# Where the second layer's residual gets its first norm's weights: inside the last output projection, or ahead of it by way of memory

## The chip, the core and the metric

The kernel runs on one core of one Trainium2 chip. The core has engines that each work through their own queue in order: PE (matmuls; PEld is its weight load), DVE (VectorE), ACT (ScalarE) and POOL (GpSimd). SP issues most DMAs, in order too; POOL issues some. The metric is the device time of one execution in microseconds (us), as a median over runs.

## The reference, cut to what matters

Two layers, each a mixer with three groups of heads and a norm behind it. 1024 tokens of 1024 values.

```
for l in range(2):
    mod = silu(c) @ w_ada[l] + b_ada[l];  shift, scale, gate = split(mod, 3)
    h = x * (1 + scale) + shift
    p = h @ w_in[l]              # latents of MLA, q k v of the dilated and the sparse heads, indexer, gates
    y = concat(MLA heads, dilated heads, sparse heads) * silu(p_gate)
    x = layer_norm(ALPHA * x + (1 + gate) * (y @ w_out[l]), ln_g[l], ln_b[l])
```

`layer_norm` takes mean and variance over the 1024 values of a token, then multiplies by `ln_g` and adds `ln_b`. The x that enters the second layer's sum is the normed x of the first layer *with* its weights: n*ln_g[0] + ln_b[0], where n is the value before weights.

## The kernel before, in words

Tokens are cut into 8 blocks of 128 (tb 7 down to 0, the order TBO). Each float32 operand is split into a high and a low part, and a product is three matmuls (high·high, low·high, high·low). A layer runs: `indexer` (keys and queries of the indexer, scores into `acc`), the dilated heads with the selection of keys beside them, the sparse heads, the latent (MLA) heads in `mla`, and `out_proj`. At the end of the first layer's `out_proj` the normed blocks n are stored to `x1_d[tb]`, transposed on PE (L876), scaled and shifted with weights folded in (`mod_h`, L366 to L371) to become h of the second layer; `mod_h` gives the low part of every odd k to POOL (L371). The stages that follow (values of the dilated heads, L377 to L384, then the indexer, from L393) read that h. The low parts of the weights that they multiply by come from POOL too (L192), and POOL issues the DMAs that copy the indexer's key to the other 64 partitions (`dup_k`, L235, L236).

In the second layer's `out_proj` (`last`), each block's n comes back from `x1_d[tb]` into a buffer of the ring XR (two buffers, L803), POOL multiplies it by ln_g[0] and adds ln_b[0] (L841, L842), PE forms the block in two halves of 512 columns of 24 matmuls each (L198), and DVE does, by halves: times the gate (L854), plus ALPHA times the residual (L855), statistics (L856); then by blocks the mean and variance (L858, L860), POOL the power (L861), DVE the norm with its weights (L865, L866), and SP the store (L867). Four sum buffers (ring X, L833) and five PSUM banks stand between PE and DVE.

The instructions are not issued in program order. A scheduler (`schedule_with_timeline_sim`, L1061) simulates the program and gives each engine a list; an instruction whose inputs are early may stand early in its engine's list, whatever its place in the text. Between engines, semaphores order the work. The names of tiles are in the views without their numbers: `acc` is the region that the rings XR and X use, `g` the other XR buffer, `bi` in L854 the gate.

Of the kernel before, what the change touches and what calls it, by code (L numbers as in the profile page):

```python
# [8 lines left out]
F32 = mybir.dt.float32  # L9
# [4 lines left out]
OP = mybir.AluOpType  # L14
# [7 lines left out]
P = 128  # L22
NB = 8
# [12 lines left out]
TBO = (7,6,5,4,3,2,1,0)  # L36
# [24 lines left out]
KE = (1,1)  # L61

NPL = 2

EARLY = (2,2)
FB = ((0,2,4,0,2,0),(1,3,1,1,1,1))
# [40 lines left out]
def trunk(ctx: ExitStack, tc: tile.TileContext, a, out):  # L107
    nc = tc.nc
    pe, act, dve, pool, sp = nc.tensor, nc.scalar, nc.vector, nc.gpsimd, nc.sync

    sb = ctx.enter_context(tc.tile_pool(name="sb", bufs=1))
# [5 lines left out]
    dr = ctx.enter_context(tc.tile_pool(name="dr", bufs=1, space=DRAM))  # L117
# [6 lines left out]
    def fresh(tag, dtype, n=1024):  # L124

        return sb.tile([P, n], dtype, name=tag, tag=tag, bufs=1)
# [4 lines left out]
    PR3 = [fresh(f"pr{i}", F32) for i in range(3)]  # L131
    PR = Halves(PR3)
    BI = Ring(fresh(f"bi{i}", F32) for i in range(2))
    G = Ring(fresh(f"g{i}", F32) for i in range(2))
    RW = Ring(fresh(f"rw{i}", F32, 512) for i in range(2))
    acc = sb.tile([P, IDX_TOT], F32, name="acc")
    AC = [acc[:, IDX_TOT - (i + 1) * 1024:IDX_TOT - i * 1024] for i in range(4)]
    scrf = sb.tile([P, 512], F32, name="scr")
    scr, scr8 = [scrf[:, i * 256:i * 256 + 256].bitcast(mybir.dt.uint8) for i in range(2)]
    o_ps = ps_o.tile([P, 2, 256], F32, name="O")  # L140

    ident = sb.tile([P, P], F32, name="ident")
    causb = sb.tile([P, 512], BF16, name="causb")
    dist2 = sb.tile([P, 2 * P], BF16, name="dist2")
# [34 lines left out]
    kr_d = dr.tile([32, 1024], F32, name="kr_d")  # L179
    g1_d = [dr.tile([1, 1024], F32, name=f"g1_d{i}") for i in range(DEPTH)]  # L180
    x1_d = [dr.tile([P, 1024], F32, name=f"x1_d{i}") for i in range(NB)]


    def bc(t):
        return t.bitcast(F32)
# [177 lines left out]
    def vblk(h):  # L363
        return lambda kb: VS[0][:, h * 1024 + kb * P:h * 1024 + (kb + 1) * P]
# [178 lines left out]
    def heads_bc(l, first, nh, gate0, y0, fill, extra=None):  # L543
# [23 lines left out]
        for h in range(nh):  # L567
            if extra:
                bias, scale = chosen, SLOPES[6 + h]
                if h == NPL:  # L570
                    PR.tiles = PR3[:]
# [105 lines left out]
    def mla(l, values):  # L677
# [8 lines left out]
        def slots(h):  # L686

            rows = [PR.tiles[(5 * h + turn.index(i)) % len(PR.tiles)] for i, _ in place]
            return [r[:, o:o + (qb + 1) * P] for qb, (r, (_, o)) in enumerate(zip(rows, place))]
# [18 lines left out]
        def keys(p):  # L708
            wh, wl = split_w(a["wuk"][l, p], 256)

            def evac(half, cols, ps):
                dve.tensor_tensor(kraw[:, cols], ps, rb[half], OP.mult)
            project(wh, wl, 2, CK, evac)
# [41 lines left out]

            project(wh, wl, 6, CA, evac)

        q, y = {}, {}
        keys(0)
        key(0)  # L760
        query(0)
# [4 lines left out]
        for h in range(6):  # L766
            if h % 2 == 0:
                y[h // 2] = G.next()
                sp.dma_start(y[h // 2], ga_d[h // 2])
            Kh, Kl = KA[h % 2]  # L770
            Qh, Ql = q[h]

            def done(g, yt=y[h // 2], yo=HA[h // 2], c=None):
                c = c or slice(g * 256, g * 256 + 256)
                act.activation(yo[0][:, c], yt[:, c], AF.Copy)
                pool.tensor_tensor(yo[1][:, c], yt[:, c], bc(yo[0][:, c]), OP.subtract)

            attend(f'A{h}', [(Qh, Kh), (Ql, Kh), (Qh, Kl)], vblk((h + 4) % 6), None, scq, y[h // 2],
                   (h % 2) * 64, ORDA[l], done if h in (3, 5) else None, PACK[l] and slots(h))
            if h < 4:  # L780
                if h % 2 == 0:
                    keys(h // 2 + 1)
                    if h == 2:
                        done(0, y[0], HA[0], slice(0, 1024))
                key(h + 2)
            for i in range(NQ[l][h], NQ[l][h + 1]):
                if i < 5:
                    query(i)

    def out_proj(l):  # L790
        last = l == DEPTH - 1
        order = [3, 4, 5, 6, 7, 0, 1, 2]
        Y = HA
        for k in order[:5]:
            raw = WR.next()
            sp.dma_start(raw, y_d[k])
            act.activation(Y[k][0], raw, AF.Copy)
            (pool if k in YP[l] else dve).tensor_tensor(Y[k][1], raw, bc(Y[k][0]), OP.subtract)


        Vs = [VS[0][:, i * 1024:(i + 1) * 1024] for i in range(6)]
        f = G.n % 2 ^ 1
        XR = Ring([AC[0]] + ([G.tiles[f]] if last else []))  # L803
        at = {3: (Vs[4], Vs[5]), 4: (Vs[0], Vs[1]), 5: W.tiles[0:2], 6: W.tiles[2:4],
              7: (fresh(f"g{1 - f}", F32R), fresh("bi1", F32R)), 0: held[0:2], 1: held[2:4],
              2: (Vs[2], [fresh(f"rw{n}", F32R, 512) for n in range(2)])}
        wo = {}
        for k in order:
            raw = WR.next()
            sp.dma_start(raw, a["w_out"][l, k])  # L810
            hi, lo = at[k]
            eng = pool if k in WP[l] else dve
            for n in range(2):
                c = slice(n * 512, n * 512 + 512)
                act.activation(hi[:, c], raw[:, c], AF.Copy)
                eng.tensor_tensor(lo[n] if k == 2 else lo[:, c], raw[:, c], bc(hi[:, c]), OP.subtract)
            wo[k] = [(hi[:, n * 512:n * 512 + 512], lo[n] if k == 2 else lo[:, n * 512:n * 512 + 512]) for n in range(2)]
        g1 = BI.tiles[0]
        sp.dma_start(g1, g1_d[l].to_broadcast([P, 1024]))
        lgb = []  # L820
        if last:
            for t, src in zip([fresh("pt0", F32), fresh("pt1", F32), PR3[2], PR3[1]],
                              (a["ln_g"][0], a["ln_b"][0], a["ln_g"][1], a["ln_b"][1])):
                sp.dma_start(t, src.to_broadcast([P, 1024]))
                lgb.append(t)
        else:

            lnc = small.tile([P, 2, 8], F32, name="lnc", bufs=1)
            sp.dma_start(lnc, a["ln_c"])
            dve.tensor_tensor(lnc[:, 0, :], lnc[:, 0, :], scale1_n, OP.mult)  # L830
            dve.tensor_tensor(lnc[:, 1, :], lnc[:, 1, :], scale1_n, OP.mult)
            dve.tensor_tensor(lnc[:, 1, :], lnc[:, 1, :], shift_n, OP.add)
        X = Ring(AC[1:4] + [PR3[0]])  # L833
        PR.tiles = [G.tiles[f]]
        xs = {}
        for tb in TBO:
            tok = slice(tb * P, (tb + 1) * P)
            xr = XR.next()
            sp.dma_start(xr, x1_d[tb] if last else a["x"][tb])
            if last:  # L840
                pool.tensor_tensor(xr, xr, lgb[0], OP.mult)  # L841
                pool.tensor_tensor(xr, xr, lgb[1], OP.add)  # L842
            r = X.next()
            st = small.tile([P, 2, 6], F32, name="st")
            for n in range(2):
                cols = slice(n * 512, n * 512 + 512)
                ps = (ps_p if n else ps_s).tile([P, 512], F32, name="pj" if n else "S")
                items = []
                for k in order:
                    yh, yl = Y[k]  # L850
                    w0, w1 = wo[k][n]
                    items += [(yh[:, tok], w0), (yl[:, tok], w0), (yh[:, tok], w1)]
                chain(ps, items)
                dve.tensor_tensor(r[:, cols], ps, g1[:, cols], OP.mult)  # L854
                dve.scalar_tensor_tensor(r[:, cols], xr[:, cols], ALPHA, r[:, cols], OP.mult, OP.add)  # L855
                dve.bn_stats(st[:, n, :], r[:, cols])  # L856
            mv = small.tile([P, 2], F32, name="mv")
            dve.bn_aggr(mv, st)  # L858
            rs = small.tile([P, 1], F32, name="rs")
            dve.tensor_scalar(rs, mv[:, 1:2], 1e-5, None, OP.add)  # L860
            pool.tensor_tensor(rs, rs, mhalf, OP.pow)  # L861
            if last:
                for n in range(2):
                    cols = slice(n * 512, (n + 1) * 512)
                    dve.scalar_tensor_tensor(r[:, cols], r[:, cols], mv[:, 0:1], lgb[2][:, cols], OP.subtract, OP.mult)  # L865
                    dve.scalar_tensor_tensor(r[:, cols], r[:, cols], rs, lgb[3][:, cols], OP.mult, OP.add)  # L866
                    sp.dma_start(out[tb][:, cols], r[:, cols])  # L867
                continue
            dve.tensor_scalar(r, r, mv[:, 0:1], rs, OP.subtract, OP.mult)
            sp.dma_start(x1_d[tb], r)  # L870
            xs[tb] = r
            if len(xs) == 4:
                for k in range(8):
                    t = ps_t.tile([P, 512], F32, name="T")
                    for j in range(4):
                        pe.transpose(t[:, j * P:(j + 1) * P], xs[tb // 4 * 4 + j][:, k * P:(k + 1) * P], ident)  # L876
                    mod_h(t, tb // 4, k, PR.next(), lnc[:, 0, :], lnc[:, 1, :])
                xs = {}
# [186 lines left out]
```

## Time and profile before

| | us |
|---|---|
| median of 3 runs | 1823.04 (1819.21 to 1823.08) |
| the profiled execution | 1825.06 |
| its span, first to last instruction | 1823.3 |
| busy in the span: PE, DVE, ACT, POOL | 1676.4 (92%), 1446.8 (79%), 1022.5 (56%), 696.9 (38%) |
| mean granted TensorE clock | 0.972 of full |

How to read it: the shares are means over stages with different limits. Near the end of the span the share of PE falls and that of POOL rises, which the forty slices of the page show as `PE ...8993` and `POOL ...6264`; ACT is at 0 in the last slices. For what a change in one stage is worth, that stage alone is read: who waits there, and for whom.

### The profile page before, as it was taken

What the parts mean: (1) busy time and instruction counts of PE and PEld (TensorE: products, weight loads), DVE (VectorE), ACT (ScalarE), POOL (GpSimd) and SP (SyncE); (2) the same over time, 40 slices, a digit from 0 to 9 for tenths busy, and PEclk for the clock granted to TensorE, in tenths of its full rate; (3) what the DMA queues carried; (4) which work ended last, traced back from release to release, by engine and by line L of the source; (5) the groups of instructions that cost most, each with busy time, mean ns of one, the idle gap of its engine ahead of it and who ended that gap; (6) DMA issues with size and microseconds to landing.
All of it is one profiled execution on the core that took longest, in us unless ns stands there. A gap on an engine that the chain in (4) does not pass through costs nothing. (4 is left out here: it accounts for less than half of the span.)

```text
span 1823.3 us, 26916 instructions
## 1 busy us (share of the span) xinstructions
PE 1676.4 (92%) x9080; PEld 1446.7 (79%) x9080; DVE 1446.8 (79%) x3510; ACT 1022.5 (56%) x2010; POOL 696.9 (38%) x625
## 2 busy tenths in 40 slices
PE   4889898999989999989999989999999899998993
PEld 4777677888887889868899978877789788986882
DVE  8889799985779678985773679999577967788589
ACT  3244477789643666575122646877974357767500
POOL 3421133333343455473322213223334346566264
PEclk9899999999999999999999999999999999999997
DMA  8465112233202441222331121232221225113222
GB/s 338 148 213 185 47 47 70 99 111 98 77 25 71 146 161 45 71 81 90 119 127 50 62 66 36 81 116 78 74 93 47 73 94 204 53 54 99 80 102 95
DMA packets 55366, 178.94 MB, mean 98 GB/s; under 512 B 7606, under 2 KB 8630, under 8 KB 54716
## 3 DMA queue, kind: packets, MB, share of 16 engines
q1 hardware_dynamic: 50812, 147.86, 24.2%
q0 software_dynamic: 4416, 29.36, 5.5%
q8 instruction: 72, 1.18, 0.3%
q14 instruction: 66, 0.54, 0.1%
HBM read 129.74 MB, written 34.87 MB: 90 GB/s over the span
## 5 line engine op out<-in xcount | busy, mean ns | idle before, releaser
L198 PE MATMUL pj<-h,w 128*128 128x512 f32 (+1 forms) x3408 | 840.0, 393 | 19.0 <-DVE qk L232 10.0
L198 PEld LDWEIGHTS pj<-h,w 128*128 128x128 f32 x3408 | 632.7, 191 | 138.2 <-issue 13.9
L198 PE MATMUL S<-qk,qk 128*128 128x512 f32 (+2 forms) x1104 | 284.1, 360 | 16.4 <-DVE mx L282 10.2
L192 POOL TENSOR_TENSOR w<-wr,w 128x1024 fp32r<-128x1024 f32 (+2 forms) x86 | 192.3, 2238 | 272.4 <-ACT w L191 258.5
L292 POOL TENSOR_SCALAR pr<-pr,den 128x896 f32<-128x896 f32 (+7 forms) x180 | 139.1, 776 | 285.4 <-DVE den L291 234.2
L318 DVE TENSOR_TENSOR pt<-T,pt 128x512 fp32r<-128x512 f32 (+1 forms) x320 | 199.8, 632 | 43.9 <-ACT pt L317 38.5
L481 ACT ACTIVATE scr<-acc,thr 128x768 uint8<-128x768 f32 x186 | 193.2, 1039 | 70.7 <-DVE thr L477 64.8
L317 ACT ACTIVATE pt<-T 128x512 fp32r<-128x512 f32 (+1 forms) x320 | 172.4, 552 | 104.4 <-PE T L314 46.3
L326 PE MATMUL O<-pt,v 128*128 128x256 f32 (+1 forms) x1280 | 215.8, 287 | 16.0 <-DVE pt L318 9.8
L198 PEld LDWEIGHTS S<-qk,qk 128*128 128x128 f32 x1104 | 184.3, 190 | 43.0 <-DVE mx L282 14.6
L326 PEld LDWEIGHTS O<-pt,v 128*128 128x128 f32 x1280 | 187.2, 192 | 36.2 <-DVE pt L318 14.8
L333 POOL TENSOR_TENSOR g<-g,osum 64x256 f32<-64x256 f32 x128 | 98.7, 771 | 224.9 <-DVE osum L331 223.4
L290 ACT ACTIVATE pr<-pr,mx 128x384 f32<-128x384 f32 (+7 forms) x188 | 145.5, 775 | 54.0 <-DVE mx L282 41.0
L461 DVE TENSOR_SCALAR_CACHE_REDUCE scr<-acc,thr 128x384 uint8<-128x384 f32 (+3 forms) x204 | 156.2, 766 | 3.2
L314 PE MATMUL T<-ident,pr 128*128 128x128 f32 x852 | 146.0, 279 | 9.2 <-POOL pr L292 5.4
L191 ACT ACTIVATE w<-wr 128x1024 fp32r<-128x1024 f32 (+2 forms) x86 | 83.9, 977 | 63.6 <-PE pj L198 58.2
L314 PEld LDWEIGHTS T<-ident,pr 128*128 128x128 f32 x852 | 102.4, 142 | 21.3 <-POOL pr L292 6.6
L198 PE MATMUL pj<-w,h 128*128 128x256 f32 (+2 forms) x672 | 108.9, 303 | 2.9 <-DVE g L241 2.0
L198 PEld LDWEIGHTS pj<-w,h 128*128 128x128 f32 x672 | 93.0, 193 | 8.0 <-DVE g L241 2.2
L435 DVE SCALAR_TENSOR_TENSOR acc<-S,wi,acc 128x512 f32<-128x512 f32 (+1 forms) x84 | 56.2, 678 | 30.7 <-ACT S L430 30.4
L330 ACT ACTIVATE osum<-O 64x256 f32<-64x256 f32 x128 | 48.6, 380 | 51.4 <-PE O L326 46.3
L282 DVE CUSTOM_DVE_ANT_0 pr<-S,bi 128x384 f32<-128x384 f32 (+2 forms) x96 | 52.2, 552 | 25.6 <-PE T L314 15.7
(274 smaller groups left out, 2625.3 us busy)
## 6 DMA issues: line engine op xcount, KB each, us to landing
wr<-in_wt_dram SPq DMA_DIRECT2D x62, 512.0 KB, 3.5
cq_d<-rw SPq DMA_DIRECT2D x64, 256.0 KB, 2.0
h<-cq_d POOLq DMA_DIRECT2D x4, 4096.0 KB, 19.6
qk<-qk POOLq DMA_DIRECT2D x48, 256.0 KB, 2.9
pt<-in_w_ada_dram SPq DMA_DIRECT2D x22, 512.0 KB, 3.9
wr<-in_w_out_dram SPq DMA_DIRECT2D x16, 512.0 KB, 3.6
bi<-in_bias_dram SPq DMA_DIRECT2D x14, 512.0 KB, 3.8
bi<-in_w_ada_dram SPq DMA_DIRECT2D x10, 512.0 KB, 4.2
```

The source lines that it names most:

```text
L191: act.activation(hi[:, :n], raw[:, :n], AF.Copy)
L192: (lo_eng or pool).tensor_tensor(lo[:, :n], raw[:, :n], bc(hi[:, :n]), OP.subtract)
L198: pe.matmul(ps, lhsT=l, rhs=r, start=(i == 0), stop=(i == len(items) - 1))
L290: act.activation(p[:, :n], p[:, :n], AF.Exp, bias=m, scale=-1.0, accum_out=den)
L292: (dve if ne[qb] else pool).tensor_scalar(p[:, :n], p[:, :n], den, 0.5, OP.mult, OP.mult)
L314: pe.transpose(t[:, c:c + P], p[j](2 * kp + kk), ident)
L317: act.activation(pt[:, 0, :n], t[:, :n], AF.Copy)
L318: dve.tensor_tensor(pt[:, 1, :n], t[:, :n], bc(pt[:, 0, :n]), OP.subtract)
L326: pe.matmul(o[:, oc], lhsT=vt(kb), rhs=pt[:, e, pc], start=(kb == 0 and e == 0), stop=(kb == 2 * g + 1 and e == 1), skip_group_check=True)
L333: pool.tensor_tensor(yc, yc, s[r0:r0 + 64], OP.mult)
L461: dve.tensor_scalar(scr8[:, :IDX_LEN[b]], scores(b), s, None, op, OP.add, accum_out=dst[:, b:b + 1])
L481: act.activation(scr[:, :IDX_LEN[b]], scores(b), AF.Sign, bias=thr[:, b:b + 1].bitcast(F32), accum_out=cnt[:, b:b + 1])
```

## The change

`residual(i)` is new. It loads one block n from `x1_d` into a new tile RES, multiplies by ln_g[0] and adds ln_b[0] on POOL (tiles LNG and LNB, new too), and stores it to a new DRAM tensor `xw_d`. `mla` calls it for the second layer: two blocks after each of the first four latent heads (NRES). The last output projection then loads from `xw_d` and has no POOL multiply and add; it loads ln_g[1] and ln_b[1] into LNG and LNB. RES joins the ring XR in both layers, so that XR has two buffers in the first layer and three in the second. To make room for three tiles of 4 KB per partition, the program's `dynamic_dma_scratch_size` is given as 4096.

```
+NRES = ((0,0,0,0,0,0),(2,2,2,2,0,0))
...
+    RES, LNG, LNB = [sb.tile([P, 1024], F32, name=n) for n in ("res", "lng", "lnb")]
...
+    xw_d = [dr.tile([P, 1024], F32, name=f"xw_d{i}") for i in range(NB)]
...
+            for _ in range(NRES[l][h]):
+                residual(rest.pop(0))
+
+    def residual(i):
+        if i == 0:
+            sp.dma_start(LNG, a["ln_g"][0].to_broadcast([P, 1024]))
+            sp.dma_start(LNB, a["ln_b"][0].to_broadcast([P, 1024]))
+        tb = TBO[i]
+        sp.dma_start(RES, x1_d[tb])
+        pool.tensor_tensor(RES, RES, LNG, OP.mult)
+        pool.tensor_tensor(RES, RES, LNB, OP.add)
+        sp.dma_start(xw_d[tb], RES)
...
-        XR = Ring([AC[0]] + ([G.tiles[f]] if last else []))
+        XR = Ring([AC[0], RES] + ([G.tiles[f]] if last else []))
...
-            sp.dma_start(xr, x1_d[tb] if last else a["x"][tb])
-            if last:
-                pool.tensor_tensor(xr, xr, lgb[0], OP.mult)
-                pool.tensor_tensor(xr, xr, lgb[1], OP.add)
+            sp.dma_start(xr, xw_d[tb] if last else a["x"][tb])
...
-    nc = bacc.Bacc("TRN2", target_bir_lowering=False, num_devices=1)
+    nc = bacc.Bacc("TRN2", target_bir_lowering=False, num_devices=1, dynamic_dma_scratch_size=4096)
```

The scheduler puts the new work elsewhere than the text does. On POOL, at the boundary of the layers, the list before has the four low parts of h (L371) in a row and then the indexer's first instructions (L404 the rotated key, L192 a weight's low part, L235 and L236 the key's copies):

```order
L371 TENSOR_TENSOR h<-g_99,h 128x512 x4
L404 TENSOR_TENSOR rw_8815<-rw_8815,pr_8813 32x512
L192 TENSOR_TENSOR w_87<-wr_92,w_86 128x1024
L235 DMA qk_82<-qk_82 64x1024
L236 DMA qk_83<-qk_83 64x1024
```

The same place of the list after (L376 is L371 of before, L409 is L404, L197 is L192, L240 is L235; L804 and L805 are the residual's multiply and add):

```order
L804 TENSOR_TENSOR res<-res,lng 128x1024
L805 TENSOR_TENSOR res<-res,lnb 128x1024
L376 TENSOR_TENSOR h<-g_99,h 128x512 x2
L804 TENSOR_TENSOR res<-res,lng 128x1024
L805 TENSOR_TENSOR res<-res,lnb 128x1024
L376 TENSOR_TENSOR h<-g_99,h 128x512 x2
L804 TENSOR_TENSOR res<-res,lng 128x1024
L805 TENSOR_TENSOR res<-res,lnb 128x1024
L804 TENSOR_TENSOR res<-res,lng 128x1024
L805 TENSOR_TENSOR res<-res,lnb 128x1024
L409 TENSOR_TENSOR rw_8826<-rw_8826,pr_8824 32x512
L804 TENSOR_TENSOR res<-res,lng 128x1024
```

Five of the eight blocks stand here, and the other three follow between the next weights' low parts; none is beside the latent heads. On SP the list after has, at the same place, a chain of load, store, load through the one tile RES (L803 the load, L806 the store; L195 a weight's load, L882 the store of the last n):

```order
L803 DMA res<-x_d_166 128x1024
L195 DMA wr_92<-in_wt_dram 128x1024
L882 DMA x_d_159<-pr_93 128x1024
L806 DMA xw_d_174<-res 128x1024
L803 DMA res<-x_d_165 128x1024
L806 DMA xw_d_173<-res 128x1024
L803 DMA res<-x_d_164 128x1024
```

Before, SP has only the store and the weights' loads there. In the last output projection POOL's list loses its sixteen L841 and L842 and keeps the eight powers. Near the start of the program SP's list gains three loads, of ln_g[0] and ln_b[0] and of a block of x into RES. In the indexers and the selections of both layers the scheduler has interleaved the same instructions in another order; from the latent heads to the end of PE's work the lists of PE agree but for a few rows.

## Rows read from the trace of the kernel before

**Rows 1.** Busy time by stretch: engines, granted clock, DMA share, GB/s

```profile
20.00:30.00 10.00, 6.41 (x22) 6.42 (x23) 9.84 (x20) 2.30 (x2) 5.51 (x3) 1.00 1.02 408
50.00:60.00 10.00, 6.75 (x31) 6.75 (x32) 9.89 (x28) 3.25 (x3) 6.95 (x3) 0.83 0.08 33
950.00:1000.00 50.00, 49.02 (x270) 46.67 (x269) 17.72 (x33) 12.99 (x24) 11.00 (x8) 1.00 0.18 46
1700.00:1750.00 50.00, 49.69 (x264) 41.83 (x263) 24.93 (x42) 16.83 (x38) 21.23 (x20) 1.00 0.21 72
1750.00:1823.00 73.00, 42.05 (x185) 34.12 (x183) 69.45 (x88) 0.00 (x0) 40.10 (x21) 0.83 0.29 101
```

**Rows 2.** The page's chain that ended last, shares by engine

```profile
DVE 3%; issue 0%; DVEq 0%
```

**Rows 3.** DVE's groups from 1740 on: count, busy us, mean ns, idle before

```profile
L855 DVE SCALAR_TENSOR_TENSOR acc<-acc 128x512 f32<-128x512 f32 x8 | 15.3, 1943 | 0.0
L866 DVE SCALAR_TENSOR_TENSOR acc<-acc,rs,pr 128x512 f32<-128x512 f32 x12 | 13.1, 1125 | 0.0
L865 DVE SCALAR_TENSOR_TENSOR acc<-acc,mv,pr 128x512 f32<-128x512 f32 x12 | 11.2, 975 | 0.0
...
L854 DVE TENSOR_TENSOR acc<-pj,bi 128x512 f32<-128x512 f32 x4 | 2.7, 675 | 6.4 <-PE pj L198 6.4
```

**Rows 4.** POOL's groups from 1740 on

```profile
L842 POOL TENSOR_TENSOR g<-g,pt 128x1024 f32<-128x1024 f32 x4 | 10.6, 2658 | 0.2
...
L841 POOL TENSOR_TENSOR acc<-acc,pt 128x1024 f32<-128x1024 f32 x4 | 10.2, 2559 | 8.0 <-DMA acc<-x_d 7.9
```

**Rows 5.** DVE in order of time, last projection: start us, duration us

```profile
1745.29 5.67 DVE L855 SCALAR_TENSOR_TENSOR acc<-acc 128x512 f32<-128x512 f32 x2
...
1814.55 0.68 DVE L854 TENSOR_TENSOR pr<-pj,bi 128x512 f32<-128x512 f32 x1
1815.26 0.69 DVE L855 SCALAR_TENSOR_TENSOR pr<-g,pr 128x512 f32<-128x512 f32 x1
...
1817.03 1.40 DVE L865 SCALAR_TENSOR_TENSOR pr<-pr,mv,pr 128x512 f32<-128x512 f32 x2
1818.35 1.40 DVE L866 SCALAR_TENSOR_TENSOR pr<-pr,rs,pr 128x512 f32<-128x512 f32 x2
```

**Rows 6.** PE in order of time, its last chain

```profile
1788.76 1.67 PE L198 MATMUL pj<-v,h 128*128 128x512 f32 x6 [2.48 <-DVE acc L854]
...
1794.14 0.39 PE L198 MATMUL pj<-rw,h 128*128 128x512 f32 x1
```

**Rows 7.** POOL in order of time at the layers' boundary

```profile
943.11 1.29 POOL L371 TENSOR_TENSOR h<-g,h 128x512 fp32r<-128x512 f32 x1 [4.42 <-ACT h L370]
...
953.02 1.29 POOL L371 TENSOR_TENSOR h<-g,h 128x512 fp32r<-128x512 f32 x1 [3.75 <-ACT h L370]
956.78 1.29 POOL L371 TENSOR_TENSOR h<-g,h 128x512 fp32r<-128x512 f32 x1 [2.48 <-ACT h L370]
...
985.36 0.61 POOL L235 DMA_DIRECT2D qk<-qk  x1
```

**Rows 8.** PE in order of time at the boundary

```profile
959.02 2.31 PE L198 MATMUL pj<-pr,h 128*128 128x392 f32 x12
962.31 2.38 PE L198 MATMUL pj<-qk,h 128*128 128x392 f32 x12 [0.98 <-DVE wi L384]
...
993.86 0.33 PE L198 MATMUL T<-qk,qk 128*128 128x384 f32 x1
```

**Rows 9.** DMA issues: transfer, count, KB each, median us to landing

```profile
qk<-qk POOLq DMA_DIRECT2D x48, 256.0 KB, 2.9
...
acc<-in_x_dram SPq DMA_DIRECT2D x8, 512.0 KB, 3.4
...
x_d<-acc SPq DMA_DIRECT2D x6, 512.0 KB, 2.6
...
bi<-in_rope_dram SPq DMA_DIRECT2D x4, 512.0 KB, 4.9
```

More of the change, by code (lines that the diff above doesn't have):

```diff
@@ L756, in query @@
             project(wh, wl, 6, CA, evac)
-        q, y = {}, {}
+        q, y, rest = {}, {}, list(range(NB))
         keys(0)
@@ L819, in out_proj @@
         sp.dma_start(g1, g1_d[l].to_broadcast([P, 1024]))
-        lgb = []
         if last:
[L822 to L825, printed above, removed]
+            sp.dma_start(LNG, a["ln_g"][l].to_broadcast([P, 1024]))
+            sp.dma_start(LNB, a["ln_b"][l].to_broadcast([P, 1024]))
         else:
@@ L864, in out_proj @@
                     cols = slice(n * 512, (n + 1) * 512)
-                    dve.scalar_tensor_tensor(r[:, cols], r[:, cols], mv[:, 0:1], lgb[2][:, cols], OP.subtract, OP.mult)
-                    dve.scalar_tensor_tensor(r[:, cols], r[:, cols], rs, lgb[3][:, cols], OP.mult, OP.add)
+                    dve.scalar_tensor_tensor(r[:, cols], r[:, cols], mv[:, 0:1], LNG[:, cols], OP.subtract, OP.mult)
+                    dve.scalar_tensor_tensor(r[:, cols], r[:, cols], rs, LNB[:, cols], OP.mult, OP.add)
                     sp.dma_start(out[tb][:, cols], r[:, cols])
```

## The prediction, written before the changed kernel was run

> **What bounds the kernel now.** I read the chain of waits first: what ended last is DVE alone, with 3% of the span [rows 2]. So I looked at the last stretch. By stretch, PE is full until 1750 (49.69 of 50 us), and from 1750 to the end it is DVE that is full, 69.45 of 73 us, while PE works 42.05 and ACT nothing [rows 1]. Before 1750 a microsecond is gained only if PE gets it; after it, only if DVE does.
>
> Then why DVE is full there. The order of time shows the same instruction at two speeds: two L855 take 5.67 us at 1745, but one takes 0.69 at 1815; two L865 or two L866 take 1.40 at the end [rows 5]. The slow ones stand where POOL works through L841 and L842, sixteen instructions of about 2.6 us, 41.8 us together [rows 4], and the last POOL instruction of that kind is over when DVE turns fast. The grouped view prices it: the 32 instructions of three groups take 15.3 + 13.1 + 11.2 = 39.6 us [rows 3]; at 0.70 each they would take 22.4. Some 17 us of DVE's time in this stage is POOL's doing, further groups of these lines not counted. L854, which reads PSUM, keeps its mean of 0.675 through it all [rows 3]. PE feels it only once, 2.48 us of waiting for a PSUM bank, and has finished at 1794.14 + 0.39 = 1794.5 [rows 6]. DVE runs 25 us longer, to 1818.35 + 1.40 = 1819.75 [rows 5].
>
> **The end, part by part.** The change takes all sixteen POOL instructions out of this stage. DVE's instructions stay, in number and shape. Per block they are two each of L854, L855, L856 at about 0.70, some 0.4 for L858 and L860, and 1.40 each for the pairs L865 and L866: 7.4 us. PE needs 24 matmuls per half, and the last half took 1788.76 to 1794.53, 5.8 us with its slow restart, so 11 us or a little more per block. DVE becomes the faster of the two. It has a backlog at 1745 (the first blocks' sums waited for L842 until 1745.3); five or six blocks' worth of work, about 44 us, is left for the 47 us in which PE finishes. I take PE as the bound of the end, with DVE only just in time. Then PE's wait of 2.48 goes, PE ends at 1794.5 - 2.5 = 1792.0, and DVE does the last half's work behind it. That tail is in the trace without any POOL beside it: from 1814.55 to 1819.75, 5.2 us. So DVE ends at 1797.3 instead of 1819.75: a gain of 22.4 us. What follows the last DVE instruction (the store and the end) stays as it is, 1823.3 - 1819.75 = 3.6 us. If instead DVE does not quite catch up, the bound is its 44 us from 1745 plus the share of the last block, 1800 at most: a gain of 19. The bounds of this term are 19 and 23; I take 22.4, since the tail's row is the same work.
>
> What is late next in that stage is nothing of the residual: the blocks come from memory by a load of 3.4 us [rows 9] into three buffers, one of which (RES) is free long before.
>
> **The boundary of the layers.** The removed work returns here, with two DMAs per block added. Sixteen POOL instructions of 2.4 to 2.7 us plus eight loads and eight stores go through one tile, so each block is a chain: load 3.4, two instructions of about 2.45, store 2.6 [rows 9]: 10.9 us a block, 87 us for eight. POOL works in order; whatever stands behind an L804 waits for its load. PE is full in this stretch, 49.02 of 50 us from 950 to 1000 [rows 1], so every wait that reaches PE counts whole.
>
> The first load can start when the first layer's last block has left RES, about 937, and lands among four other loads, say at 941.5. L804 and L805 then end at 946.4, and the first low part of h runs after them instead of at 943.11 [rows 7]. The second residual's load may start only after the first's store: 946.4 + 2.6 + 3.4 = 952.4, its two instructions end at 957.3, and only then comes the third low part, which before ran at 953.02. It ends at 958.6, its buffer goes to the fourth, and that ends near 961.7 where before it was 956.78 + 1.29 = 958.07. PE wants these last two parts from about 958, and before it began the last group of that product at 959.02 and was through at 961.33, with 0.98 of waiting after it [rows 8]. The delay that reaches PE is 1 to 2 us.
>
> Next, POOL must issue the copies of the indexer's key, before at 985.36 [rows 7]; PE wants them at 993.86 [rows 8]. After, the fifth residual's L804 stands ahead of the first copy and its L805 between the two. Four and a half periods of 10.9 from 941.5 put the second copy's issue at about 992 to 994, its landing 2.9 later at 995 to 997 [rows 9]. PE by then is 1 to 2 us late itself, so the cost here is 0 to 2 us. The weights' low parts behind it have over 5 us of slack. Bounds for the whole boundary: 0 if everything hides, and with loads of 4.9, as the slowest row of that size has it [rows 9], and POOL at 2.7, a period of 13 us, which brings 5 us at the low parts and up to 5 more at the copies: 10. I take 3.
>
> The same effect can hurt here. DVE makes four low parts of h at the boundary itself; if each were stretched from 0.69 to 2.84 (half of 5.67) as an L855 is beside POOL [rows 5], that is 8.6 us more of DVE's time. I add none of it: by the chain above DVE is waiting for POOL's low part in any case, and its other work there reads PSUM, as L854 does [rows 3]. The Trainium skill ("SBUF — State Buffer", section "Who interferes with whom") states the rule that speaks against the change here: a DVE instruction with two inputs in SBUF contends with a GpSimd instruction that reads SBUF, and one with at most one such input doesn't. By that rule the four low parts would be held up and the total would be 8.6 higher, 1812; by the rows on who waits for whom it stays out of the sum.
>
> **Smaller edits.** Three loads of 512 KB more near the start, where the DMA engines are full (share 1.02 at 408 GB/s from 20 to 30 us), are 3.9 us of transfer; by 50 to 60 us the share is 0.08 [rows 1], so the queue drains long before. DVE is the full engine there (9.84 and 9.89 of 10). Cost 0, up to 4 if that cover were gone. A second buffer for x in the first layer's projection: PE is full there, 0. The other interleaving in the indexers and selections: no row prices it; 0, with 4 either way as the spread that the three runs have by themselves (1819.21 to 1823.08).
>
> **The sum.** Span 1823.3 - 22.4 + 3 = 1803.9 us. The median of the runs is 0.26 below the profiled span (1823.04 against 1823.3; the profiled execution itself took 1825.06), so the forecast is 1803.6 us.
>
> **The rivals.** First, the boundary costs more: loads land at 4.9 instead of 3.4, or DVE's four low parts are stretched one after the other, on the path to PE. For it: PE has no slack there. Against: DMA share is only 0.18. Either gives the 10 us of the bound or a little less instead of 3: 1803.6 + 7 = 1811. Second, DVE stays the bound of the end: it does not catch up its backlog, because each block's L866 waits for POOL's power. For it: 44 us of work against 47 is thin. It gives 19 instead of 22.4 or a little less, 1807 to 1810. Third, slower than before: the boundary eats the whole gain. The place is POOL's queue between the low parts of h and the key's copies. The second copy lands at 941.5 + 4.5 periods + 3.5, and PE wanted it at 995; a loss of 26 us, which would make the kernel slower by over 0.2%, needs a period of about 17 us per block, 1827 or more. No transfer of this size and no POOL instruction in the rows is long enough for that. Fourth, and also slower: the smaller scratch makes POOL's own DMAs wait for their predecessors to land. There are 48 copies with a landing of 2.9 [rows 9]; if half of these waits reached PE, the time would be 1803.6 + 70 = 1873. It decides from the point where a second copy's issue takes as long as a landing; today an issue takes 0.61 [rows 7]. The Trainium skill ("SBUF — State Buffer", section "SBUF size: 192, 224, or 256?") puts this scratch at 16 KiB, the ring of descriptors for DMAs that GpSimd issues; no run here shows what a fourth of it does. Last, the interleaving elsewhere brings or takes several us, which a single forecast can't know.
>
> **How the numbers follow.** The forecast, with the boundary at 0 to 6 and the end at 21 to 23, has 0.58 and its own range of 1800 to 1808. The dear boundary has 0.16, DVE as the bound 0.10, a lucky interleaving below 1800 0.06, an end in no measurable difference 0.04 (dear boundary and unlucky interleaving together), the boundary that eats everything 0.04, the scratch 0.02. The range that leaves out about 2 in 10 is 1797 to 1815. Within 0.2% (3.6 us), about what a measurement here can tell from no change, I put 0.04; slower 0.06; faster 0.90.
>
> **What would show it.** Right: in the changed kernel's last stage L855, L865 and L866 are all near 0.70, POOL has only the powers there, PE's last chain ends with no wait for a bank, and DVE ends about 5 us after PE instead of 25. At the boundary POOL's L804 waits for `res` from memory, and PE waits a few us for a low part of h or for the key's copy. Wrong: DVE is still busy more than 10 us behind PE; PE loses more than 10 us between 940 and 1030; copies issued by POOL take several us to issue.

## The result, and the profile after

| | before | after |
|---|---|---|
| median, us | 1822.13 (4 runs, 1819.21 to 1823.08) | 1798.31 (4 runs, 1795.74 to 1800.83) |
| profiled execution / its span, us | 1825.06 / 1823.3 | 1795.81 / 1794.0 |
| mean granted clock | 0.972 | 0.981 |

The ratio is 0.9876, 95% interval 0.9857 to 0.9895: the changed kernel is faster by 23.8 us in the medians. The forecast was 1803.6, its range 1797 to 1815. The four runs of the changed kernel lie in two pairs, two at 1795.8 and two at 1800.8; the trace is of one of the first pair.

What ended last in the changed kernel (the page's chain of waits, shares by engine) is no longer DVE alone, as in [rows 2]:

```profile
PE 49%; DVE 34%; ACT 7%; issue 6%; DMA 4%; POOL 1%; DVEq 0%; ACTq 0%; SPq 0%; POOLq 0%
```

By stretch (columns as in [rows 1]; the last stretch ends with the span):

```profile
950.00:1000.00 50.00, 48.55 (x261) 45.35 (x260) 15.80 (x30) 13.94 (x26) 30.77 (x17) 1.00 0.39 129
1700.00:1750.00 50.00, 49.69 (x259) 41.77 (x258) 33.72 (x61) 11.57 (x24) 12.45 (x15) 1.00 0.23 75
1750.00:1794.00 44.00, 35.63 (x158) 29.19 (x156) 32.11 (x57) 0.00 (x0) 4.62 (x6) 0.94 0.27 95
```

After 1750 DVE works 32.11 us of 44 where it worked 69.45 of 73, and POOL 4.62 where it worked 40.10. The DVE groups from 1735 on (L866 is L854 of before, L867 is L855, L868 is L856, L877 is L865, L878 is L866) are all at about 0.7 us, which [rows 3] had at up to 1.9 in the mean:

```profile
L878 DVE SCALAR_TENSOR_TENSOR acc<-acc,rs,lnb 128x512 f32<-128x512 f32 x12 | 8.5, 742 | 0.0
L877 DVE SCALAR_TENSOR_TENSOR acc<-acc,mv,lng 128x512 f32<-128x512 f32 x12 | 8.4, 746 | 0.0
...
L867 DVE SCALAR_TENSOR_TENSOR acc<-g,acc 128x512 f32<-128x512 f32 x4 | 2.7, 691 | 0.0
L867 DVE SCALAR_TENSOR_TENSOR acc<-res,acc 128x512 f32<-128x512 f32 x3 | 2.1, 693 | 0.0
```

From 1737.5 on POOL has only the powers, and is idle before them:

```profile
L873 POOL TENSOR_TENSOR rs<-rs,mhalf 128x1 f32<-128x1 f32 x8 | 7.6, 952 | 44.4 <-DVE rs L872 44.2
```

PE in order of time, its last instruction; there is no wait for a bank from 1738 on, where [rows 6] had one of 2.48:

```profile
1785.24 0.39 PE L203 MATMUL pj<-rw,h 128*128 128x512 f32 x1
```

And DVE behind it, in order of time:

```profile
1785.67 0.69 DVE L866 TENSOR_TENSOR pr<-pj,bi 128x512 f32<-128x512 f32 x1 [3.29 <-PE pj L203]
1786.39 0.69 DVE L867 SCALAR_TENSOR_TENSOR pr<-res,pr 128x512 f32<-128x512 f32 x1
...
1789.48 1.41 DVE L878 SCALAR_TENSOR_TENSOR pr<-pr,rs,lnb 128x512 f32<-128x512 f32 x2
```

DVE waits 3.29 us for PE's last chain and ends at 1790.89, 5.3 us behind PE's 1785.63 (before: 25).

The stage also begins otherwise. Before, DVE stood idle for 6.44 us, and its first L855 began at 1745.29 [rows 5], right behind the end of POOL's first L842 (1742.86 + 2.40); PE's last matmuls of the heads' sums had begun 9.1 us earlier, at 1736.18. After, the first L867 begins 0.9 us ahead of those matmuls (1730.10). Before and after:

```profile
1744.60 0.69 DVE L854 TENSOR_TENSOR acc<-pj,bi 128x512 f32<-128x512 f32 x1 [6.44 <-PE pj L198]
```

```profile
1729.23 0.87 DVE L867 SCALAR_TENSOR_TENSOR acc<-acc 128x512 f32<-128x512 f32 x1
```

At the boundary of the layers, POOL in order of time (L804 and L805 the residual, L376 a low part of h, L240 and L241 the key's copies):

```profile
934.59 2.39 POOL L804 TENSOR_TENSOR res<-res,lng 128x1024 f32<-128x1024 f32 x1 [1.69 <-DMA res<-x_d]
937.05 2.40 POOL L805 TENSOR_TENSOR res<-res,lnb 128x1024 f32<-128x1024 f32 x1
...
945.63 2.38 POOL L804 TENSOR_TENSOR res<-res,lng 128x1024 f32<-128x1024 f32 x1 [0.35 <-DMA res<-x_d]
948.09 2.72 POOL L805 TENSOR_TENSOR res<-res,lnb 128x1024 f32<-128x1024 f32 x1
950.76 1.29 POOL L376 TENSOR_TENSOR h<-g,h 128x512 fp32r<-128x512 f32 x1
953.65 1.28 POOL L376 TENSOR_TENSOR h<-g,h 128x512 fp32r<-128x512 f32 x1 [1.59 <-ACT h L375]
957.44 2.38 POOL L804 TENSOR_TENSOR res<-res,lng 128x1024 f32<-128x1024 f32 x1 [2.51 <-DMA res<-x_d]
...
984.37 0.61 POOL L240 DMA_DIRECT2D qk<-qk  x1
985.00 2.42 POOL L805 TENSOR_TENSOR res<-res,lnb 128x1024 f32<-128x1024 f32 x1
987.36 0.55 POOL L241 DMA_DIRECT2D qk<-qk  x1
```

PE in the same stretch:

```profile
955.03 2.30 PE L203 MATMUL pj<-pr,h 128*128 128x392 f32 x12
958.31 2.39 PE L203 MATMUL pj<-qk,h 128*128 128x392 f32 x12 [0.98 <-DVE wi L389]
...
992.13 0.44 PE L203 MATMUL T<-qk,qk 128*128 128x384 f32 x1 [0.41 <-DMA qk<-qk]
```

The period of the blocks is 11 to 12 us (934.59, 945.63, 957.44), as worked out, and the work does run through POOL ahead of PE's operands. The third low part, at 950.76, stood behind an L805, and DVE waited for it:

```profile
952.09 0.81 DVE L374 TENSOR_SCALAR g<-T,lnc 128x512 f32<-128x512 f32 x1 [0.76 <-POOL h L376]
```

So the last low part, at 953.65, waited for ACT, ACT for DVE and DVE for POOL. Counted from the start of the transposes of the first layer's last four blocks (L888 at 936.03, L876 before at 940.02), it began at 17.6 us, where it had begun at 16.8. PE lost nothing by it: the group of twelve at 955.03 begins 19.0 us behind that mark, as the one at 959.02 did before. The wait of 0.98 us on PE was there before [rows 8], and the only new one is 0.41 us for a key's copy (0.95 in two waits when the kernel was traced again). Issuing a copy takes 0.55 to 0.61 us, as in [rows 7].

One number misleads. The transposes begin at 936.03 here and began at 940.02 before, so this execution is 4 us ahead where the change has hardly begun. I first took that for a gain of the other interleaving; the runs below say otherwise.

### The profile page after: what moved, and what is told of

Read it like the earlier page. It is cut to its first block, busy times and chain, and to the rows that moved or that the text cites. A ratio compares the mean times of both kernels' runs of the same rounds, so it can differ in the third digit from the quotient of the medians.

```text
span 1794.0 us, 26935 instructions
## 1 busy us (share of the span) xinstructions
PE 1672.8 (93%) x9080; PEld 1440.7 (80%) x9080; DVE 1421.7 (79%) x3510; ACT 1019.1 (57%) x2010; POOL 699.1 (39%) x625
## 4 chain that ended last, share of the span: by engine, by line
PE 49%; DVE 34%; ACT 7%; issue 6%; DMA 4%; POOL 1%; DVEq 0%; ACTq 0%; SPq 0%; POOLq 0%
PE pj L203 28%; PE S L203 11%; DVE scr L466 6%; PE O L331 5%; PE T L319 4%; DVE pt L323 3%; DVE g L925 3%; ACT scr L486 3%; DVE pr L287 3%; DMA h<-cq_d 2%; DVE thr L482 1%; DVE acc L440 1%; DVE g L260 1%; DVE qk L237 1%; DVE osum L336 1%
## 5 line engine op out<-in xcount | busy, mean ns | idle before, releaser
L197 POOL TENSOR_TENSOR w<-wr,w 128x1024 fp32r<-128x1024 f32 (+2 forms) x86 | 193.6, 2252 | 248.6 <-ACT w L196 239.1
L297 POOL TENSOR_SCALAR pr<-pr,den 128x896 f32<-128x896 f32 (+7 forms) x180 | 139.7, 779 | 272.7 <-DVE den L296 200.2
L331 PE MATMUL O<-pt,v 128*128 128x256 f32 (+1 forms) x1280 | 216.9, 287 | 15.5 <-DVE pt L323 10.3
L331 PEld LDWEIGHTS O<-pt,v 128*128 128x128 f32 x1280 | 188.2, 192 | 37.1 <-DVE pt L323 15.8
L338 POOL TENSOR_TENSOR g<-g,osum 64x256 f32<-64x256 f32 x128 | 98.9, 773 | 230.2 <-DVE osum L336 228.8
L336 DVE TENSOR_TENSOR osum<-O,osum 64x256 f32<-64x256 f32 x128 | 53.4, 417 | 23.1 <-ACT osum L335 19.4
```

Source lines behind the costliest of these rows:

```text
L197: (lo_eng or pool).tensor_tensor(lo[:, :n], raw[:, :n], bc(hi[:, :n]), OP.subtract)
L297: (dve if ne[qb] else pool).tensor_scalar(p[:, :n], p[:, :n], den, 0.5, OP.mult, OP.mult)
L331: pe.matmul(o[:, oc], lhsT=vt(kb), rhs=pt[:, e, pc], start=(kb == 0 and e == 0), stop=(kb == 2 * g + 1 and e == 1), skip_group_check=True)
L338: pool.tensor_tensor(yc, yc, s[r0:r0 + 64], OP.mult)
```

## The experiments

Times vary by some us between executions of one kernel, so in each trace I took one mark: *a*, the start of PE's last eight matmuls of the heads' sums (`O<-pt,v`, L331, L326 before). In the five traces whose last stage holds the same work (after, after_again, end_only, res_none, res_pool4) what follows it is equal to 0.02 us. All kernels, in us:

| run | median (runs) | ratio to before, interval | a | PE's end after a | DVE's end after a |
|---|---|---|---|---|---|
| before | 1822.13 (4) | | 1736.18 | 58.35 | 83.57 |
| after | 1798.31 (4) | 0.9876, 0.9857 to 0.9895 | 1730.10 | 55.53 | 60.79 |
| after_again | 1799.30 (4) | 0.9886, 0.9873 to 0.9900 | 1735.01 | 55.53 | 60.78 |
| end_only | 1801.01 (4) | 0.9881, 0.9867 to 0.9895 | 1735.07 | 55.54 | 60.80 |
| pool_beside | 1819.10 (11) | 0.9988, 0.9977 to 0.9999 | 1736.41 | 64.32 | 80.75 |
| pool_one | 1851.21 (5) | 1.0176, 1.0161 to 1.0190 | 1731.44 | 55.54 | 87.10 |
| both_places | 1817.78 (7) | 0.9975, 0.9964 to 0.9985 | 1731.55 | 59.83 | 80.15 |
| ring_l1 | 1818.96 (12) | 0.9984, 0.9974 to 0.9994 | 1739.02 | 58.49 | 80.35 |
| ring_l0 | 1826.53 (12) | 1.0026, 1.0016 to 1.0036 | 1735.74 | 58.33 | 83.63 |
| res_none | 1799.77 (5) | 0.9881, 0.9864 to 0.9898 | 1737.77 | 55.54 | 60.80 |
| res_pool4 | 1801.88 (4) | 0.9890, 0.9874 to 0.9906 | 1737.04 | 55.53 | 60.79 |
| res_mla | 1818.28 (12) | 0.9978, 0.9966 to 0.9989 | 1755.40 | 52.59 | 57.85 |

Each ratio is to runs of the kernel before on the same chip. Beside the row before, their medians were 1822.17 (end_only, pool_beside, both_places, ring_l0), 1822.76 (ring_l1 and the three with res) and 1819.75 (after_again, pool_one), so medians of different chips can be off against each other by 3 us; the ratios are not.

**end_only: the sixteen instructions alone.**

```
             sp.dma_start(xr, x1_d[tb] if last else a["x"][tb])
-            if last:
-                pool.tensor_tensor(xr, xr, lgb[0], OP.mult)
-                pool.tensor_tensor(xr, xr, lgb[1], OP.add)
```

> The kernel before, with only the sixteen POOL instructions (times ln_g[0], plus ln_b[0]) of the last output projection left out, so that the residual is n without its weights; nothing is put in their place, the residual's work at the layers' boundary is absent, and PE's list is that of before. Theory (POOL beside DVE is the whole of the end's loss): DVE's L855, L865 and L866 all near 0.70 us, DVE ends about 5 us behind PE instead of 25, and the time is 1822 - 25 = 1797 us (1795 to 1801). Rival A (a part of the gain comes from elsewhere, the other interleaving in the first layer, or the third buffer for the residual): 1801 to 1806, DVE's instructions fast all the same. Rival B (DVE stays behind for another reason): 1807 or more.

Measured 1801.01, a gain of 21.2, on the border of theory and rival A. The last stage has all that the changed kernel's has: 60.80 us from *a* against 60.79. Its DVE groups from 1735 on:

```profile
L863 DVE SCALAR_TENSOR_TENSOR acc<-acc,rs,pr 128x512 f32<-128x512 f32 x12 | 8.9, 783 | 0.0
L862 DVE SCALAR_TENSOR_TENSOR acc<-acc,mv,pr 128x512 f32<-128x512 f32 x12 | 8.8, 770 | 0.0
...
L852 DVE SCALAR_TENSOR_TENSOR acc<-acc 128x512 f32<-128x512 f32 x8 | 5.6, 705 | 0.1
```

The L852 (L855 before) went from 15.3 us to 5.6 for the same eight [rows 3]. The 25 in the expectation was too much; the stage gives 83.57 - 60.80 = 22.8.

**pool_beside: the same POOL work, with nobody waiting for its product.** The kernel after, with this in its last projection (D is a tile that nobody reads):

```
+            D = fresh("pt0", F32)
...
             xr = XR.next()
             sp.dma_start(xr, xw_d[tb] if last else a["x"][tb])
+            if last:
+                pool.tensor_tensor(D, xr, LNG, OP.mult)
+                pool.tensor_tensor(D, D, LNB, OP.add)
```

> The kernel after, with sixteen POOL instructions of the same kind and size added in the last projection: they read the loaded residual and write a tile that nobody reads, so DVE does not wait for their result. Theory (it is POOL's work beside DVE that slows DVE's instructions with two inputs in SBUF): those instructions go from 0.70 back to 1.5 to 2.8 us, DVE ends more than 15 us behind PE, time 1798 + 15 to 22 = 1813 to 1820 us. Rival (before, DVE was late because it waited for the product of POOL): DVE's instructions stay near 0.70 and the time is 1798 to 1801.

Measured 1819.10: of the gain 3.1 us are left, as the theory had it. Which instructions are hit, from the DVE groups from 1735 on (L871 is L855 of before, L881 is L865, L882 is L866) and then in order of time:

```profile
L882 DVE SCALAR_TENSOR_TENSOR acc<-acc,rs,lnb 128x512 f32<-128x512 f32 x12 | 29.1, 2470 | 0.0
L881 DVE SCALAR_TENSOR_TENSOR acc<-acc,mv,lng 128x512 f32<-128x512 f32 x12 | 10.3, 894 | 0.0
```

```profile
1752.06 11.34 DVE L882 SCALAR_TENSOR_TENSOR acc<-acc,rs,lnb 128x512 f32<-128x512 f32 x4
...
1792.61 0.69 DVE L871 SCALAR_TENSOR_TENSOR acc<-g,acc 128x512 f32<-128x512 f32 x1
```

Four L882 take 11.34 us, 2.84 each, half of the 5.67 for two in [rows 5]; in this order of work it is mostly the L882 that meet POOL, in [rows 3] it was mostly the L855. No wait of DVE shows from 1740 on, and PE waits 5.28 us for it at one place, which its end of 64.32 shows. So POOL at work beside DVE is the cause of 80.75 - 60.79 = 20.0 us in this stage, with no product awaited. The other 2.8 us up to 83.57 go with the third buffer: with it (ring_l1, below) the stage is 80.35 although the product is awaited there.

What happens to such an instruction can be read from single ones. In the kernel before, three DVE instructions began at different points of a POOL instruction:

```profile
1777.62 1.69 DVE L866 SCALAR_TENSOR_TENSOR acc<-acc,rs,pr 128x512 f32<-128x512 f32 x1
1779.83 2.28 DVE L866 SCALAR_TENSOR_TENSOR acc<-acc,rs,pr 128x512 f32<-128x512 f32 x1
...
1800.05 2.70 DVE L855 SCALAR_TENSOR_TENSOR acc<-acc 128x512 f32<-128x512 f32 x1
```

```profile
1776.22 2.54 POOL L842 TENSOR_TENSOR acc<-acc,pt 128x1024 f32<-128x1024 f32 x1
1778.72 2.85 POOL L841 TENSOR_TENSOR g<-g,pt 128x1024 f32<-128x1024 f32 x1
...
1799.28 2.93 POOL L841 TENSOR_TENSOR g<-g,pt 128x1024 f32<-128x1024 f32 x1 [2.04 <-DMA g<-x_d]
```

They took 1.69, 2.28 and 2.70 us, and each ended 0.54 or 0.55 us behind the end of the POOL instruction in which it began (1778.76, 1781.57, 1802.21). The same 0.55 holds for every DVE instruction of this kind that began inside such a POOL instruction in the last stages of before, pool_beside, both_places, ring_l0 and ring_l1, 70 in all. Those that began before POOL's took 0.63 to 0.75. So DVE is not slowed to a quarter: it is held until POOL's instruction is over, and 2.84 is what it costs to begin right behind the start of one.

**pool_one: POOL kept busy by instructions with one input.** The edit is against pool_beside:

```
             if last:
-                pool.tensor_tensor(D, xr, LNG, OP.mult)
-                pool.tensor_tensor(D, D, LNB, OP.add)
+                for _ in range(4):
+                    pool.tensor_scalar(D, xr, 1.5, None, OP.mult)
```

> The kernel after, with POOL kept at work in the last projection by another kind of instruction: per block four multiplications by a constant (one input in SBUF, 128x1024 into a tile nobody reads) where the kernel with POOL beside had a multiply and an add of two inputs. Theory (DVE's two-input instructions lose to any POOL instruction that reads SBUF, in proportion to its time): DVE's instructions at 1.5 to 2.8 us beside them, 1806 to 1818 us. Rival (only POOL instructions of two inputs take so much): DVE's near 0.70, 1798 to 1801 us.

Both missed on the time, 1851.21, since I had taken such an instruction to be short. It takes 2.83 us, four of them 11.3 per block, and each block's buffer is free only behind them: POOL is the bound. DVE waits 6.8 us at a time for a load, and after DVE's end POOL works on to 1844.7. What can be read from it is how long DVE's instructions take beside such work. DVE in order of time:

```profile
1745.91 1.40 DVE L882 SCALAR_TENSOR_TENSOR acc<-acc,rs,lnb 128x512 f32<-128x512 f32 x2
...
1760.95 1.59 DVE L882 SCALAR_TENSOR_TENSOR pr<-pr,rs,lnb 128x512 f32<-128x512 f32 x2
...
1789.25 2.19 DVE L882 SCALAR_TENSOR_TENSOR acc<-acc,rs,lnb 128x512 f32<-128x512 f32 x2
...
1798.19 1.74 DVE L871 SCALAR_TENSOR_TENSOR acc<-acc 128x512 f32<-128x512 f32 x2 [6.76 <-DMA acc<-xw_d]
```

and POOL beside it:

```profile
1744.97 2.77 POOL L858 TENSOR_SCALAR pt<-acc 128x1024 f32<-128x1024 f32 x1
...
1760.18 2.90 POOL L858 TENSOR_SCALAR pt<-res 128x1024 f32<-128x1024 f32 x1
...
1789.08 5.74 POOL L858 TENSOR_SCALAR pt<-acc 128x1024 f32<-128x1024 f32 x2
```

Two of DVE's two-input instructions take 1.40 to 2.19 beside these, against 5.67 beside POOL's two-input ones. A pair that begins 0.17 us behind the start of a POOL instruction takes 2.19, one at 0.77 takes 1.59, and one at 0.94 takes 1.40, as without POOL, though that POOL instruction runs on for 1.8 us. So here DVE is held only near the start of POOL's instruction, and not to its end; why was not tried further.

**both_places and ring_l1: the added work alone, and the third buffer alone.** The first is the kernel after with the last projection of before (the tiles for the four vectors are those of before too, not shown):

```
...
-            sp.dma_start(xr, xw_d[tb] if last else a["x"][tb])
+            sp.dma_start(xr, x1_d[tb] if last else a["x"][tb])
+            if last:
+                pool.tensor_tensor(xr, xr, lgb[0], OP.mult)
+                pool.tensor_tensor(xr, xr, lgb[1], OP.add)
```

> The kernel after, with its residual work at the layers' boundary and its list on PE, and in the last projection again the load of n, the sixteen POOL instructions and the tiles of before (the result of the boundary's work is stored and not read). Theory (boundary costs PE 0.4 us, the other interleaving of the first layer brings 4): 1822 - 3.6 = 1818.5 us, PE's key project of the indexer at 967 as in the kernel after. Rival A (my prediction's sum: boundary 3, interleaving 0): 1825. Rival B (the lead of 4 us is only the spread of single executions): 1822.

The second is the kernel before with one edit besides the new tile and the smaller scratch:

```
-        XR = Ring([AC[0]] + ([G.tiles[f]] if last else []))
+        XR = Ring([AC[0]] + ([RES, G.tiles[f]] if last else []))
```

> The kernel before, with the smaller scratch, one tile more, and that tile only as the third buffer of the residual's ring in the second layer's last projection; PE's list is that of before. Theory (the 4.4 us that the kernel with the work in both places gained are mainly the third buffer, since its last stage was 3.4 us shorter in the profile): 1822 - 3.5 = 1818.5 us. Rival A (they are the interleaving of the first layer): 1822, no change. Rival B (the smaller scratch costs something at POOL's own transfers): above 1826.

Measured 1817.78 and 1818.96, 4.4 and 3.8 below before. The third buffer doesn't let POOL begin sooner (4.6 us behind *a* in ring_l1, 4.2 before), but its last add ends sooner (62.3 against 68.8), and the last stage is shorter by 83.57 - 80.35 = 3.2 us as long as POOL has work in it; with that taken out, both_places is within about 1 us of before. So all the work at the boundary costs nothing that shows in the median, and neither does the scratch: the rival in which it makes the copies wait did not come about. The theory on ring_l1 held; that on both_places had the right number for a wrong reason.

**ring_l0: the other interleaving of the first layer.** The kernel before, again with the new tile and the smaller scratch:

```
-        XR = Ring([AC[0]] + ([G.tiles[f]] if last else []))
+        XR = Ring([AC[0]] + ([G.tiles[f]] if last else [RES]))
```

> The kernel before, with the smaller scratch and one tile more, and that tile only as the second buffer for x in the first layer's last projection; the last projection of the second layer is that of before. The list of PE in the first layer begins as in the kernel after and has about as many moved rows. Theory (the lead of 4 us that the kernel after has at the layers' boundary comes from the interleaving that this buffer brings): the transposes of the first layer's end stand at 936 instead of 940 and the time is 1818 us. Rival A (the lead is from another edit, or from the spread of single executions): 1822. Rival B (each interleaving is a draw of its own): anywhere from 1816 to 1828, with no relation to the lead of the kernel after.

The theory fell: 1826.53, 4.4 us *slower* than before, though its profiled execution reached the boundary at 935.17, earliest of all. Rival B is what is left: the scratch costs nothing (ring_l1), so the 4.4 us are those of the second x buffer with the interleaving that it brings; the two were not separated. And the mark at the boundary is no property of a list: the kernel after, run again, has it at 940.38 instead of 936.03.

**after_again: the kernel after, timed again.**

> The kernel after, unchanged, timed in more rounds, since its four first runs lie at 1796 and 1801 us and the pieces to be told apart are of 3 us. Theory (the end brings 21 us, as the kernel before without its sixteen POOL instructions shows with 1801; boundary and interleaving bring 1 to 3 more): 1798 to 1800 us. Rival (the rest beyond the end is chance of four runs): 1801 to 1802.

1799.30 (1798.83 to 1800.73). Against its own chip the kernel after stands at 0.9876 and 0.9886, end_only at 0.9881, between the two. The time is in the range of the theory, but its premise, 1 to 3 us from boundary and interleaving, does not show beyond the end.

**res_none and res_pool4: none of the boundary's work, and more of it.** Both are edits of the kernel after; in res_none the last projection loads n from `x1_d` besides (not shown).

```
...
-            for _ in range(NRES[l][h]):
-                residual(rest.pop(0))
```

> The kernel after, with the residual's work at the layers' boundary left out (no loads, no POOL instructions, no stores; the last projection reads n, without the first norm's weights). PE's list is that of after through the whole first layer, and otherwise interleaved in parts of the second. Theory (the boundary's work is hidden but for 0.4 us): 1798 us, with the 2 or 3 us that another interleaving can bring either way. Rival (my term of 3 us for the boundary): 1795 us.

```
         pool.tensor_tensor(RES, RES, LNB, OP.add)
+        pool.tensor_tensor(RES, RES, LNG, OP.mult)
+        pool.tensor_tensor(RES, RES, LNB, OP.add)
```

> The kernel after, with each block's POOL work at the boundary doubled: multiplied by ln_g[0] and added ln_b[0] a second time, four POOL instructions instead of two, so the residual's values are others. PE's list is that of after but for seven moved rows; on POOL the two copies of the indexer's key now stand behind the third block's work and not within the fifth's. Theory (PE loses only where a low part of h or a key's copy is late; with blocks every 16 us the fourth low part comes about 1 us late and the copies in time): 1798 to 1800 us. Rival (every microsecond of POOL at the boundary that is in front of PE's operands counts, as the term of 3 us in the prediction had it; 16 further instructions of 2.4 us): 1803 to 1818.

Without it the ratio is 0.9881 (1799.77), with it 0.9876 and 0.9886, with twice the POOL work 0.9890 (1801.88). So 39 us more of POOL move the time by 0.7 to 2.6 us, less than the width of one interval, and the boundary's own work by nothing that shows; the intervals alone would leave room for about 4 us either way. The traces are narrower. Between 930 and 1040 PE's new waits, all for the key's copies, are 0.41 us (after), 0.95 (after_again) and 1.01 (res_pool4), and none in res_none. From the boundary's transposes to *a* it is 793.1 to 797.2 us in five kernels with the boundary's work (after, after_again, both_places, pool_beside, pool_one), 795.9 to 800.6 in five without it (before, end_only, res_none, ring_l0, ring_l1). The price of the boundary as the change has it is under 1 us of waiting in PE. So the theory on res_none held, and 1801.88 for res_pool4 lies between theory and rival.

**res_mla: the residual truly beside the latent heads.** In the change, the call stands among the latent heads and the work runs at the boundary, since the scheduler takes what is ready. So here each load is made to wait for the current head (yt is the tile of its sum):

```
...
+        pool.tensor_tensor(RES[:, 0:64], yt[:, 0:64], yt[:, 0:64], OP.mult)
         sp.dma_start(RES, x1_d[tb])
```

> The kernel after, with a small POOL instruction (64 columns of the current latent head's sum into RES) ahead of each residual load, so that the load can't start before that head: the eight blocks now stand truly beside the latent heads, POOL and DVE both at work there. PE's list is that of after through the first layer. Theory (what costs is POOL beside a DVE that is the bound; among the latent heads PE is full and DVE has slack, so the price is small but not nothing, since the heads' sums also wait in POOL's queue): 1800 us, 1797 to 1805. Rival (POOL beside DVE's two-input instructions stretches what PE waits for, as in the last projection): 1808 or more.

The theory fell and the rival held: 1818.28, nearly the whole gain lost, and all of it ahead of *a* (1755.40, where the others have 1730 to 1739). It is lost beside the residual: the first of its loads is issued at 1599.4; the 1161st matmul into `O` starts at 1603.6 here and at 1602.9 in after_again, the 1241st at 1680.5 and 1668.5. The stretch 1650 to 1700 in this kernel:

```profile
1650.00:1700.00 50.00, 37.64 (x191) 29.65 (x191) 35.75 (x85) 29.41 (x64) 42.14 (x40) 0.83 0.39 132
```

and in the kernel after, which is 10 to 20 us further on in its work there:

```profile
1650.00:1700.00 50.00, 46.99 (x280) 39.34 (x280) 41.64 (x109) 35.50 (x80) 25.65 (x33) 0.98 0.23 76
```

POOL has 42.14 us of 50 against 25.65, and PE, DVE and ACT all do less; the granted clock is 0.83 against 0.98. Waits in res_mla from 1600 to 1740 (engine, line, waited for: us in total, times, longest), and a DVE low part that took 3.80 us:

```profile
POOL res L805 <- DMA res<-x_d: 12.4, 7, 5.1
...
ACT acc L295 <- POOL acc L297: 4.5, 2, 2.5
```

```profile
1671.86 3.80 DVE L835 TENSOR_TENSOR w<-wr,w 128x512 fp32r<-128x512 f32 x1 [1.51 <-ACT w L834]
```

The heads need POOL in turn for each block (L297 scales the probabilities, L338 adds the sums), and behind an L805 they wait for its load and then for its work. How the 17 to 19 us (0.9978 against 0.9886 and 0.9876) divide between that queue, the held DVE instructions, the clock and the other interleaving was not separated.

## Why the prediction was right, point by point

- **The end, forecast 22.4.** Right in mechanism and size. The last stage, from *a* to DVE's end, fell by 83.57 - 60.79 = 22.8 us: PE's share is 58.35 - 55.53 = 2.8 (forecast 2.5, the wait alone; its slow restart came on top) and the tail behind PE is 5.26 (forecast 5.2). end_only shows that the sixteen instructions are the whole of it, pool_beside that 20.0 of it is their work beside DVE. What the prediction read as a second speed is a hold to the end of POOL's instruction; the 17 us that it put on three groups are 25 over all of the 48 L855, L865 and L866.
- **DVE "only just in time".** This step failed, without harm to the number. The backlog of 44 us at 1745 was kept for the changed kernel, but it was POOL's doing too: the first L867 begins at 1729.23, 0.9 us before *a*, where the first L855 began 9.1 us behind it. DVE waits 3.29 us for PE's last chain, and the rival in which DVE stays the bound had no ground.
- **The boundary, forecast +3.** The mechanism was put right (a chain of 11 us a block, low parts behind it, copies late) and the size was wrong: 0.41 to 0.95 us of new waiting in PE, nothing that shows in the median (res_none). What failed is the start of the chain. I let the first load land at 941.5 among other loads; it landed 1.4 us before that execution's transposes of the last four blocks began (934.59 against 936.03), where I had it 1.5 us behind them (941.5 against 940.02). So the last low part came 0.9 us later than before and not 3.6 (961.7 against 958.07), and PE's group began at its old place: the 1 to 2 us for the low parts were 0. The copies were late by the 0.41 to 0.95. The upper bound of 10 rested on a misreading: 4.9 is the slowest load among [rows 9], but the trace has loads of 512 KB at 6.4 (`acc<-in_w_ad_dram`) and 9.6 (`v<-in_xt_dram`).
- **DVE's low parts beside POOL, costed at 0.** Three of the four at the boundary took 0.68 to 0.79 and one 1.82 us, which ended 0.55 us behind an L805; PE did not wait for any. The rule of the Trainium skill that I weighed there ("SBUF — State Buffer", section "Who interferes with whom") is borne out by the hold in pool_beside. At this place it cost 1.2 us of DVE's time and not 8.6, since the other three low parts met no such POOL instruction, or only its last 0.2 us.
- **Startup, second x buffer, scratch at 0.** Scratch and startup: no cost in both_places and ring_l1. The second x buffer moves the first layer's lists, and by itself it cost 4.4 us (ring_l0); in the changed kernel, with other lists again, nothing of that shows. "0, 4 either way" was the right size for it.
- **The sum.** Forecast 1823.3 - 22.4 + 3; the runs give -22.8 and under 1. That is 1799.3 from 1822.1, without the boundary, where the two medians are 1798.31 and, on a chip on which before is 2.4 lower, 1799.30. Of the 4.3 us between 1799.3 and the forecast of 1803.6, 3 are the boundary's term, 0.9 the median of before (1823.04 then) and 0.4 the end. What is left to the measured 1798.31 is about 1 us, within the spread of the runs.
- **The rivals.** The boundary that eats the gain needed a period of 17 us: res_pool4 has periods of 17.3 us and more (its L804 begin at 937.50, 954.88 and 972.16) and loses 2.6 at most; but its list has the key's copies behind the third block's work and not within the fifth's, so it isn't that rival's case in full. It exists in another place: res_mla is the same work, with eight small POOL instructions more, and loses the gain.

## What to carry to other kernels

POOL's work is not free because POOL is idle: price it by what stands beside it, and move it to where DVE has slack and PE's operands either do not pass through POOL or have time to wait. The place is what the engine's list says and not where the call stands; the same eight blocks cost nothing that shows at the boundary and about 18 us among the heads. To judge pieces of a few us, measure from a mark inside the trace: here whole executions of one kernel differ by 5 us, and the last stage of its two traces by 0.01.

## What the runs showed of the hardware

DVE's instruction of 128x512 float32 with two inputs in SBUF takes 0.70 us alone. Begun during a POOL instruction of two inputs, it ends 0.55 us behind that one's end, so it takes up to 2.9 us; begun before it, it takes its usual time, and POOL's 2.39 us for 128x1024 become up to 2.93. Beside POOL's one-input instructions a pair took 1.40 to 2.19, by how close behind their start it began. A one-input POOL instruction of 128x1024 took 2.83 us with DVE at rest, more than one of two inputs alone (2.39). DVE's statistics and its instructions that read PSUM keep 0.67 to 0.69 in the mean beside either (pool_beside, pool_one).
